# The input projection of a two-layer trunk in three sections of columns, its weights in quarters

## The chip, the cores and the metric

The kernel runs on one core of one Trainium2 chip. The metric is the device time of one execution in microseconds (us); smaller is better. On the core, TensorE (PE in the profile) multiplies matrices, VectorE (DVE), ScalarE (ACT) and GpSimd (POOL) work element by element, and SyncE (SP) issues most of the DMA transfers. Each engine takes its instructions strictly in the order in which they stand in its own queue.

## What is computed

The reference is a trunk of two layers. Each layer mixes tokens with four groups of heads side by side (latent attention, neighbourhood attention "natten", a bidirectional S5 state space model, and retention) and then runs a mixture of experts. There are 512 latent and 256 context tokens, 1024 wide. What matters here is one product in each layer: the normed tokens times `w_in`, whose columns feed all four mixers.

```
hl = rmsnorm(x)   * (1 + scale) + shift      # 512 latent tokens, 1024 wide
hc = rmsnorm(ctx) * (1 + scale) + shift      # 256 context tokens
pl = split_cols(hl @ w_in[layer])            # cq 192 | ckv 128 | kr 32 | natten q,k,v | u | retention q,k,v,g
pc = split_cols(hc @ w_in[layer])
...
s5: state h[t] = abar * h[t-1] + bbar u[t], both directions; y = Re(c h) + d u; gelu; gated by w_glu
```

## The kernel before

**Tokens and columns.** A tile of tokens is 128 rows; there are six (`NT`), four latent and two context. The 1376 columns that are wanted with tokens on the partitions (`nat_ps` in the profile) are made in five sections, `SECS = (0, 288, 560, 832, 1104, 1376)`. `proj_nat(s, ...)` (line 515) makes one section: for each tile of tokens it accumulates 8 slices of the contraction (`KD`, 128 each) in one bank of PSUM, three matmuls for each slice, because the product is made from a high and a low part of each operand (`mm3`, lines 201 to 203). That is 24 matmuls for a tile and section; the number of columns in the section is the number of columns that each matmul streams. In layer 1 the context tokens need no queries, so their tiles begin at a later column: at `N_KR` in section 0 (32 columns), at `N_NV` in section 1 (80 columns), and at the section's start elsewhere. The remaining columns (u, and natten's q and k, and retention's gate) are made transposed (`tr_ps`, `proj_tr`): u before the sections, the others after them.

**Weights.** `wload` (line 488) brings one half of a section's weights, 512 of the 1024 rows of the contraction, into `w_raw`; `wnext` (line 499) casts it on ACT (`w_hi`, line 195), takes the rest by a subtraction on POOL (`w_lo`, line 196), and issues the load of the same half of the next section. There are three buffers of `w_raw` and four each of `w_hi` and `w_lo`, so two whole sections fit: the next one is ready while one is used.

**What is done with a section's tile.** DVE or ACT copies it out of PSUM (`evac`, lines 189 and 191). For cq and ckv there is a normalisation: ACT squares and sums, DVE makes `rs_a` (line 223), POOL makes `rs_b` (line 225), DVE scales into `acn` (line 1038), PE transposes that (`a_t`, lines 1041 and 1043). Three banks of PSUM serve `nat_ps` and `tr_ps`.

**S5 among the sections.** `s5_states` (line 763) is emitted after section 0 and `s5_out` after section 2 (`S5AT`). `s5_states` first makes the inputs of a scan with 64 small matmuls (`s5_v`, line 777), for which eight tiles `Fg` are loaded into two buffers. ACT copies them into `H`, and then DVE runs the scan: 56 operations on 192 columns (lines 789 to 792), 88 on 16 columns (797 to 800), 8 on 1232 columns (805 to 808). When it ends, ACT copies `H` to `HP` (lines 814 to 816). `s5_out` multiplies `HP` with tables (`s5_y`, lines 835 to 837; 92 of its 96 matmuls stand behind the first use of `HP`), copies to `Y`, loads a table and applies gelu on ACT (839), writes `Y` to memory and reads it back as `GT` (842, 844), DVE adjusts it (845), and PE multiplies it with `w_glu` (`s5_z`, line 857).

**What sets the order.** A scheduler in the framework orders the instructions of each engine when the program is built, by its own model of cost, within what the data and buffers allow. So the position of an instruction in its queue is fixed then, and a changed tile size moves other instructions too.

Of the kernel before, what the change touches and what calls it, by code (L numbers as in the profile page):

```python
# [9 lines left out]
F32 = mybir.dt.float32  # L10
F32R = mybir.dt.float32r
# [7 lines left out]
P = 128  # L19
# [14 lines left out]
SECS = (0, 288, 560, 832, 1104, 1376)  # L34
# [95 lines left out]
N_RQ, N_KR, N_CQ, N_NV, N_CKV, N_NW, N_RK, N_RV = 0, 256, 288, 480, 560, 688, 864, 1120  # L130
# [3 lines left out]
_ORDER = ("rq", "kr", "cq", "nv", "ckv", "nw", "rk", "rv", "u", "nq", "nk", "rg")  # L134
# [29 lines left out]
class Trunk:  # L164

    NB = ((7, 4, 3), (7, 6, 0))
    S5AT = ((0, 2), (0, 2))
# [156 lines left out]
    def mixer(self, l):  # L324
        tc, nc = self.tc, self.nc
        nt = self.nt
        with ExitStack() as left, ExitStack() as right:
            mS = self.pool("mS", es=left)
            self.mxS = mS.tile([P, 2, 2, nt * P], F32R, name="mixS")
            with ExitStack() as proj:  # L330
# [44 lines left out]
                with ExitStack() as sx:  # L375
                    na = self.pool("na", 2, es=sx, side="right")
                    self.s5u = self.pool("s5u", es=sx, side="right")
                    w = self.wnext()
                    self.s5_in(w, natP, self.s5u)
                    self.mla_prep_load(na)  # L380
                    for s in range(5):
                        self.proj_nat(s, na, tabs)
                        if s == self.S5AT[l][0]:
                            for _ in tabs:
                                pass
                            tb.close()
                            s5p, s5w = self.pool("s5p", es=sx, side="right"), self.pool("s5w", 2, es=sx, side="right")
                            self.s5_states(s5p, s5w)
                        if s == self.S5AT[l][1]:
                            self.s5_out(s5p, s5w)  # L390
# [97 lines left out]
    def wload(self, c0, w, a):  # L488

        r = self.W.tile([P, 4, w], F32, tag="raw", name="w_raw", bufs=3)  # L490
        o = c0 * D + a * 512 * w
        self.nc.sync.dma_start(out=r.rearrange("p k n -> p (k n)"), in_=self.I["w_in"][self.l, o:o + 512 * w].rearrange("(p n) -> p n", p=P))
        return r

    def wstart(self):
        self.secs = [(T_U, 256)] + [(a, b - a) for a, b in zip(SECS[:-1], SECS[1:])] + [(T_NK, 256), (T_RG, 256), (T_NQ, 256)]
        self.ahead = [self.wload(*self.secs[0], a) for a in range(2)]

    def wnext(self):

        w = self.secs.pop(0)[1]
        his, los, ahead = [], [], []
        for a in range(2):
            hi = self.W.tile([P, 4, w], F32R, tag="whi", name="w_hi", bufs=4)
            lo = self.W.tile([P, 4, w], F32R, tag="wlo", name="w_lo", bufs=4)
            self.split(hi, lo, self.ahead[a], self.nc.gpsimd)
            if self.secs:
                ahead.append(self.wload(*self.secs[0], a))
            for k in range(4):
                his.append(hi[:, k])  # L510
                los.append(lo[:, k])
        self.ahead = ahead
        return his, los

    def proj_nat(self, s, na, side):
# [5 lines left out]
        for i in range(NT):  # L521

            a = c0 if (i < LAT or self.need_ctx) else (N_KR, N_NV, c0, c0, c0)[s]
# [6 lines left out]
            next(side, None)  # L530
            next(side, None)
            for p0, w, dst in ((N_RQ, 256, self.nat[:, i, 0]), (N_KR, 32, None), (N_CQ, 192, None), (N_NV, 80, 0), (N_CKV, 128, None),
# [11 lines left out]
                elif dst is None:  # L544
                    g = self.mla_prep(i, p0, src, na)
                    next(g)
                    self.later.append(g)
                else:
                    self.evac(dst[:, x0 - p0:x1 - p0], src)

# [1328 lines left out]
def _layout(i):  # L1879
# [7 lines left out]
    r["w_in"] = np.concatenate([w[:, :, x:y].reshape(L, 2, 4, P, y - x).transpose(0, 1, 3, 2, 4).reshape(L, -1) for x, y in zip(cuts[:-1], cuts[1:])], axis=-1)  # L1887
# [40 lines left out]
```

## Time and profile before

| | us |
|---|---|
| median of three runs (2271.03 to 2276.7) | 2274.34 |
| the profiled execution | 2264.39 |
| span of its trace | 2262.6 |
| PE busy in the span | 1965.2 (87%) |
| DVE busy | 944.2 (42%) |
| POOL busy | 366.5 (16%) |
| the 1440 matmuls of nat_ps, busy | 146.6 + 144.0 + 144.2 |
| layer 0: first nat_ps matmul to first natten score | 89.94 to 297.15 |
| layer 1: the same | 1284.62 to 1476.61 |

Times inside the execution are counted from the start of the span. The profiled execution is 10 us below the median. A matmul's busy time in the trace includes the part in which the next one already runs, so what a row of matmuls takes is read from starts, not from busy times.

### The profile page before, as it was taken

How to read it: one execution, taken by the hardware profiler on the slowest of the kernel's cores; microseconds unless marked ns; L12 is line 12 of the kernel's file. 1: busy time of each engine (PE TensorE's matmuls, PEld its weight loads, DVE VectorE, ACT ScalarE, POOL GpSimd, SP SyncE). 2: the span in 40 equal slices, each digit the busy share in tenths (PEclk: the TensorE clock that was granted, in tenths of full speed). 3: DMA queues.
4: the chain of work that ended last, by engine and by line, in shares of the span. 5: the costliest groups of instructions: out<-in, count | busy, mean ns of one | idle time of the engine just before them, and what ended most of it. 6: DMA issues, size and time to landing. Idle time of an engine off the chain costs nothing. (4 is left out here: it accounts for less than half of the span.)

```text
span 2262.6 us, 32559 instructions
## 1 busy us (share of the span) xinstructions
PE 1965.2 (87%) x12449; PEld 1157.3 (51%) x12449; DVE 944.2 (42%) x2178; ACT 502.9 (22%) x1099; POOL 366.5 (16%) x396
## 2 busy tenths in 40 slices
PE   5887988899779899899887878988996999989996
PEld 2787765467633333333222778855574444444443
DVE  4757156463525411111112447166534444544445
ACT  3442232351202110000001432232522011111111
POOL 2431252220110000000003222262302000000000
PEclk8899999999879999999998989989996899999998
DMA  7441355753468999999998421365544899999996
GB/s 271 112 145 43 92 173 190 220 172 119 177 257 303 356 385 374 378 382 385 406 379 322 134 82 42 83 201 172 191 157 156 315 382 378 389 420 419 420 387 260
DMA packets 160476, 578.53 MB, mean 256 GB/s; under 512 B 30032, under 2 KB 71504, under 8 KB 111152
## 3 DMA queue, kind: packets, MB, share of 16 engines
q1 hardware_dynamic: 123344, 530.69, 62.0%
q10 hardware_dynamic: 31296, 31.36, 4.4%
q0 software_dynamic: 5664, 14.23, 2.2%
q8 instruction: 103, 1.69, 0.3%
q14 instruction: 69, 0.57, 0.1%
HBM read 536.33 MB, written 43.42 MB: 256 GB/s over the span
## 5 line engine op out<-in xcount | busy, mean ns | idle before, releaser
L1670 PE MATMUL e_pa<-ew,hT 128*64 128x512 f32 x1792 | 451.9, 605 | 36.1 <-DMA ew<-in_moe_w 29.9
L1670 PEld LDWEIGHTS e_pa<-ew,hT 128*64 128x64 f32 x1792 | 137.5, 139 | 312.7 <-issue 259.2
L1694 PE MATMUL e_py<-ew,aT 128*64 128x512 f32 x896 | 219.4, 625 | 10.1 <-DVE aT L1686 8.9
L225 POOL TENSOR_TENSOR rs_b<-rs_a,mhalf 128x1 f32<-128x1 f32 (+1 forms) x58 | 38.3, 660 | 854.6 <-PE po_ps L1639 513.5
L1675 ACT ACTIVATE sA<-e_pa 64x512 f32<-64x512 f32 x56 | 33.1, 591 | 597.8 <-PE e_pa L1670 580.7
L201 PE MATMUL nat_ps<-w_hi,hTh 128*128 128x272 f32 (+3 forms) x480 | 146.6, 305 | 8.3 <-ACT nat L189 6.5
L1676 DVE TENSOR_TENSOR sA<-sA,e_pa 64x512 f32<-64x512 f32 x56 | 38.6, 690 | 274.5 <-ACT sA L1675 273.9
L203 PE MATMUL nat_ps<-w_hi,hTl 128*128 128x272 f32 (+3 forms) x480 | 144.2, 300 | 0.0
L202 PE MATMUL nat_ps<-w_lo,hTh 128*128 128x272 f32 (+3 forms) x480 | 144.0, 300 | 0.0
L196 POOL TENSOR_TENSOR w_lo<-w_raw,w_hi 128x1024 fp32r<-128x1024 f32 (+2 forms) x36 | 90.2, 2517 | 231.0 <-DMA w_raw<-in_w_in 108.5
L1694 PEld LDWEIGHTS e_py<-ew,aT 128*64 128x64 f32 x896 | 62.1, 142 | 120.5 <-issue 105.0
L191 DVE COPY hT<-hg_t 128x256 f32<-128x256 f32 (+2 forms) x46 | 24.7, 537 | 199.8 <-PE e_pa L1670 166.3
L1556 POOL DMA_INDIRECT hg<-hd,stok x32 | 30.7, 960 | 443.8 <-PE hg_t L1568 368.4
L295 PE MATMUL mod_ps<-wmod,cT 128*32 128x256 f32 x768 | 77.0, 429 | 28.4 <-DMA wmod<-in_w_mod 28.4
L201 PEld LDWEIGHTS nat_ps<-w_hi,hTh 128*128 128x128 f32 x480 | 95.8, 200 | 10.5 <-ACT nat L189 7.9
L202 PE MATMUL tr_ps<-hTl,w_hi 128*128 128x256 f32 (+1 forms) x256 | 88.6, 346 | 10.0 <-POOL hTl L485 9.0
L202 PEld LDWEIGHTS nat_ps<-w_lo,hTh 128*128 128x128 f32 x480 | 95.7, 199 | 0.4 <-issue 0.4
L203 PEld LDWEIGHTS nat_ps<-w_hi,hTl 128*128 128x128 f32 x480 | 95.4, 199 | 0.2 <-issue 0.2
L201 PE MATMUL tr_ps<-hTh,w_hi 128*128 128x256 f32 (+1 forms) x256 | 88.2, 344 | 5.1 <-DVE gT L582 3.3
L203 PE MATMUL tr_ps<-hTh,w_lo 128*128 128x256 f32 (+1 forms) x256 | 85.8, 335 | 0.0
L1641 DVE TENSOR_TENSOR xr<-xr,po_ps 128x512 f32<-128x512 f32 x112 | 72.3, 684 | 7.9 <-PE po_ps L1639 7.4
L1016 PE MATMUL pT_ps<-const,sm_p 128*128 128x128 f32 x352 | 56.2, 286 | 18.4 <-DVE sm_p L1006 11.8
(471 smaller groups left out, 3495.3 us busy)
## 6 DMA issues: line engine op xcount, KB each, us to landing
ew<-in_moe_w SPq DMA_DIRECT2D x384, 1024.0 KB, 11.1
wmod<-in_w_mod SPq DMA_DIRECT2D x96, 512.0 KB, 4.5
yd<-zero SPq DMA_DIRECT2D x20, 512.0 KB, 5.0
w_raw<-in_w_in SPq DMA_DIRECT2D x16, 544.0 KB, 4.5
w_raw<-in_w_in SPq DMA_DIRECT2D x16, 512.0 KB, 3.2
w_raw<-in_w_out SPq DMA_DIRECT2D x32, 256.0 KB, 3.4
yd<-yA ACTq DMA_DIRECT2D x64, 128.0 KB, 6.1
hd<-h ACTq DMA_DIRECT2D x10, 512.0 KB, 2.6
```

Source lines behind the costliest of these rows:

```text
L196: (eng or self.nc.vector).tensor_tensor(out=lo, in0=src, in1=_f(hi), op=ALU.subtract)
L201: mm(out, lhsT=lh, rhs=rh, start=start, stop=False)
L202: mm(out, lhsT=lh, rhs=rl, start=False, stop=False)
L203: mm(out, lhsT=ll, rhs=rh, start=False, stop=stop)
L225: nc.gpsimd.tensor_tensor(out=r, in0=t, in1=self.mhalf[:, :n], op=ALU.pow)
L295: nc.tensor.matmul(ps[32 * j:32 * j + 32, 256 * q:256 * q + 256], lhsT=self.cT[:, k], rhs=w[:, j], start=(k == 0), stop=(k == KD - 1))
L1016: nc.tensor.transpose(pt[:, b], p[:, (a + b) * P:(a + b + 1) * P], self.ident)
L1641: nc.vector.tensor_tensor(out=x, in0=x, in1=ps, op=ALU.add)
L1670: mm(pa[64 * j:64 * j + 64], lhsT=hT[k][:, 0:64], rhs=(w1, w3)[j][k], start=(k == 0), stop=(k == KD - 1))
L1675: nc.scalar.activation(out=sA, in_=pa[0:64], func=AF.Silu)
L1676: nc.vector.tensor_tensor(out=sA, in0=sA, in1=pa[64:128], op=ALU.mult)
L1694: mm(py[64 * j:64 * j + 64, 0:512], lhsT=aT[:, k * 64:(k + 1) * 64], rhs=w2[k][:, h * 512:(h + 1) * 512], start=(k == 0), stop=(k == 3))
```

## The change

The five sections become three, of 464, 464 and 448 columns. The columns are put in another order: those of natten's w (`N_NW`, 176) move up beside `rq` and `kr`. In layer 1 the context tiles now stream 208, 272 and 448 columns where they streamed 32, 80, 272, 272 and 272.

Weights are loaded, cast and subtracted in quarters of the contraction, two slices each, four per section instead of two. `w_raw` keeps three buffers, `w_hi` has five and `w_lo` six, each half as deep and about 1.6 times as wide; so a section and one or two quarters fit, and not two sections. The generator that makes S5's tables between the tiles is advanced three times for a tile instead of twice. `s5_states` is emitted after tile 3 of section 0, `s5_out` after tile 4 of section 1.

```diff
-SECS = (0, 288, 560, 832, 1104, 1376)
+SECS = (0, 464, 928, 1376)
...
-N_RQ, N_KR, N_CQ, N_NV, N_CKV, N_NW, N_RK, N_RV = 0, 256, 288, 480, 560, 688, 864, 1120
+N_RQ, N_KR, N_NW, N_CQ, N_NV, N_CKV, N_RK, N_RV = 0, 256, 288, 464, 656, 736, 864, 1120
...
-    S5AT = ((0, 2), (0, 2))
+    S5AT = ((0, 3), (1, 4))
...
-        r = self.W.tile([P, 4, w], F32, tag="raw", name="w_raw", bufs=3)
-        o = c0 * D + a * 512 * w
+        r = self.W.tile([P, 2, w], F32, tag="raw", name="w_raw", bufs=3)
+        o = c0 * D + a * 256 * w
...
-        for a in range(2):
-            hi = self.W.tile([P, 4, w], F32R, tag="whi", name="w_hi", bufs=4)
-            lo = self.W.tile([P, 4, w], F32R, tag="wlo", name="w_lo", bufs=4)
+        for a in range(4):
+            hi = self.W.tile([P, 2, w], F32R, tag="whi", name="w_hi", bufs=5)
+            lo = self.W.tile([P, 2, w], F32R, tag="wlo", name="w_lo", bufs=6)
...
-            a = c0 if (i < LAT or self.need_ctx) else (N_KR, N_NV, c0, c0, c0)[s]
+            a = c0 if (i < LAT or self.need_ctx) else (N_KR, N_NV, c0)[s]
...
-            next(side, None)
-            next(side, None)
+            for _ in range(3):
+                next(side, None)
...
+            then(s, i)
```

`then(s, i)` holds the two calls that stood behind the sections: `s5_states` where `(s, i) == (0, 3)` and `s5_out` where `(s, i) == (1, 4)`. Lines behind the first edits move by one to four.

**PE, layer 0, where `HP` is first used.** `nat_ps` are section tiles, `tr_ps` the transposed ones behind all sections. Before:

```order
L203 MATMUL nat_ps_2480<-w_hi_2364,hTl_94 128x272
L201 MATMUL nat_ps_2480<-w_hi_2364,hTh_93 128x272
L202 MATMUL nat_ps_2480<-w_lo_2365,hTh_93 128x272
L836 MATMUL s5_y_2029<-HP_1503,Eg_2016 128x96
L203 MATMUL nat_ps_2480<-w_hi_2364,hTl_94 128x272
```

Now:

```order
L202 MATMUL tr_ps_2276<-hTh_93,w_hi_2252 128x512
L203 MATMUL tr_ps_2276<-hTl_94,w_hi_2252 128x512
L204 MATMUL tr_ps_2276<-hTh_93,w_lo_2253 128x512
L840 MATMUL s5_y_1855<-HP_1487,Eg_1842 128x96
L202 MATMUL tr_ps_2276<-hTh_93,w_hi_2258 128x512
```

Before, 40 section matmuls stood behind the first use of `HP`; now all sections stand ahead of it.

**DVE, layer 1, where the scan begins.** The first operation of the scan is the one that reads `H` and `s5pw1`. Before:

```order
L1038 TENSOR_SCALAR acn_11457<-nat_ps_11426,rs_b_11461 128x192
L191 COPY nv_11464<-nat_ps_11426 128x80
L223 TENSOR_SCALAR rs_a_11500<-ass_11497 128x1
L1038 TENSOR_SCALAR acn_11498<-nat_ps_11467,rs_b_11502 128x192
L789 TENSOR_TENSOR rt_11178<-H_11097,s5pw1_7513 128x192
```

Now:

```order
L1062 TENSOR_TENSOR kr_10442<-nat_ps_10784,k_krc_10647 128x32
L1064 TENSOR_TENSOR krt_10810<-nat_ps_10784,k_krs_10649 128x2x8 x2
L192 COPY nv_10816<-nat_ps_10784 128x176
L1065 TENSOR_TENSOR kr_10442<-kr_10442,krt_10810 128x32
L793 TENSOR_TENSOR rt_10906<-H_10825,s5pw1_7255 128x192
```

Before, the scan stood behind three tiles of section 1; now it stands behind the fourth tile of section 0, ahead of all of section 1.

**POOL, layer 1, towards the end of the scan.** The `memset` of `HP` waits for the scan's last operation. Before:

```order
L225 TENSOR_TENSOR rs_b_11808<-rs_a_11806,mhalf_59 128x1
L196 TENSOR_TENSOR w_lo_12195<-w_raw_12009,w_hi_12194 128x1088
L225 TENSOR_TENSOR rs_b_11847<-rs_a_11845,mhalf_59 128x1
L196 TENSOR_TENSOR w_lo_12201<-w_raw_12015,w_hi_12200 128x1088
L812 MEMSET HP_11367 64x16
```

Now:

```order
L226 TENSOR_TENSOR rs_b_11390<-rs_a_11388,mhalf_59 128x1
L197 TENSOR_TENSOR w_lo_11638<-w_raw_11176,w_hi_11637 128x896
L197 TENSOR_TENSOR w_lo_11644<-w_raw_11182,w_hi_11643 128x896
L197 TENSOR_TENSOR w_lo_11650<-w_raw_11188,w_hi_11649 128x896
L197 TENSOR_TENSOR w_lo_11825<-w_raw_11635,w_hi_11824 128x512
L816 MEMSET HP_11095 64x16
```

Three quarters of the last section (`w_lo_11638` and the two behind it) now stand behind the `rs_b` of the last latent tile of the section before, and directly ahead of the scan's end.

## Rows read from the trace of the kernel before

**Rows 1.** Stretches: us, busy us (instructions) by engine, clock, DMA share, GB/s.

```profile
152.70:216.70 64.00, 51.29 (x378) 49.17 (x378) 59.75 (x173) 11.87 (x35) 12.98 (x10) 0.97 0.23 73
219.80:265.90 46.10, 45.73 (x297) 41.18 (x298) 2.78 (x4) 13.59 (x18) 11.76 (x8) 1.00 0.37 92
...
1334.20:1399.80 65.60, 51.41 (x368) 50.21 (x368) 60.52 (x176) 12.47 (x41) 14.12 (x11) 0.87 0.17 51
...
1403.00:1476.00 73.00, 71.97 (x434) 62.81 (x434) 8.49 (x11) 21.12 (x31) 19.09 (x12) 1.00 0.32 83
```

**Rows 2.** What PE waited for, 89.9 to 297.2: total us, times, longest.

```profile
PE a_t L1041 <- DVE acn L1038: 6.7, 5, 2.5
...
PE s_t L727 <- DVE G L707: 3.4, 1, 3.4
```

**Rows 3.** The same, 1284.6 to 1477.

```profile
PE a_t L1041 <- DVE acn L1038: 11.9, 3, 8.5
PE s_v L777 <- DMA Fg<-s5f: 6.0, 2, 4.4
```

**Rows 4.** DVE, layer 0's scan: start, duration, operation, [idle before it, releaser].

```profile
152.76 0.51 DVE L789 TENSOR_TENSOR rt<-H,s5pw 128x192 f32<-128x192 f32 x1 [0.42 <-ACT H L782]
...
172.05 0.35 DVE L1038 TENSOR_SCALAR acn<-nat_ps,rs_b 128x128 f32<-128x128 f32 x1 [0.43 <-POOL rs_b L225]
172.32 2.58 DVE L792 TENSOR_TENSOR H<-H,rt 128x192 f32<-128x192 f32 x1
...
215.15 1.44 DVE L808 TENSOR_TENSOR H<-H,fx 128x1232 f32<-128x1232 f32 x1
```

**Rows 5.** POOL in order of time, the same moment.

```profile
172.00 2.49 POOL L196 TENSOR_TENSOR w_lo<-w_raw,w_hi 128x1088 fp32r<-128x1088 f32 x1
```

**Rows 6.** POOL's subtractions by shape: count, busy us, mean ns, idle before.

```profile
L196 POOL TENSOR_TENSOR w_lo<-w_raw,w_hi 128x1088 fp32r<-128x1088 f32 x16 | 41.2, 2585 | 34.0 <-ACT w_hi L195 34.0
L196 POOL TENSOR_TENSOR w_lo<-w_raw,w_hi 128x1024 fp32r<-128x1024 f32 x16 | 38.0, 2383 | 197.0 <-DMA w_raw<-in_w_in 108.5 <-ACT w_hi L195 70.8 <-PE nat_ps L203 10.4
```

**Rows 7.** PE in order of time: two first matmuls of tiles following each other.

```profile
212.96 0.29 PE L201 MATMUL nat_ps<-w_hi,hTh 128*128 128x272 f32 x1
215.98 0.29 PE L201 MATMUL nat_ps<-w_hi,hTh 128*128 128x272 f32 x1
1453.65 0.39 PE L201 MATMUL tr_ps<-hTh,w_hi 128*128 128x512 f32 x1
1459.09 0.39 PE L201 MATMUL tr_ps<-hTh,w_hi 128*128 128x512 f32 x1
```

**Rows 8.** PE, layer 1: first and last matmul of a tile of 32 columns.

```profile
1297.41 0.18 PE L201 MATMUL nat_ps<-w_hi,hTh 128*128 128x32 f32 x1
1299.90 0.26 PE L203 MATMUL nat_ps<-w_hi,hTl 128*128 128x32 f32 x1
```

**Rows 9.** DVE, start of layer 1's scan.

```profile
1334.26 0.55 DVE L789 TENSOR_TENSOR rt<-H,s5pw 128x192 f32<-128x192 f32 x1 [2.66 <-ACT H L782]
```

**Rows 10.** The tile Fg: last line of its page of instructions.

```profile
DMA to landing us min/median/max: 2.8/3.0/3.8
```

**Rows 11.** ACT and PE: from the last s5_y to s5_z in layer 0, and beyond.

```profile
248.38 0.48 ACT L838 COPY Y<-s_y 128x384 f32<-128x384 f32 x1 [6.62 <-PE s_y L837]
265.91 0.56 PE L857 MATMUL s_z<-GT,wglu 128*128 128x384 f32 x1 [0.38 <-DVE GT L845]
275.33 0.39 PE L201 MATMUL tr_ps<-hTh,w_hi 128*128 128x256 f32 x1 [3.32 <-DVE gT L582]
279.43 0.63 PE L201 MATMUL tr_ps<-hTh,w_hi 128*128 128x512 f32 x1
```

**Rows 12.** PE: first use of HP in each layer, and layer 1's first natten score.

```profile
219.76 0.43 PE L836 MATMUL s_y<-HP,Eg 128*128 128x96 f32 x2 [2.61 <-issue]
1402.96 0.32 PE L836 MATMUL s_y<-HP,Eg 128*128 128x96 f32 x1 [1.58 <-issue]
1476.61 0.48 PE L1146 MATMUL n_s<-nkT,nqT 64*128 64x256 f32 x1 [0.69 <-ACT nqT L587]
```

More of the change, by code (lines that the diff above doesn't have):

```diff
@@ L133 @@
                rq=(1376, 256), rk=(1632, 256), rv=(1888, 256), rg=(2144, 256))
-_ORDER = ("rq", "kr", "cq", "nv", "ckv", "nw", "rk", "rv", "u", "nq", "nk", "rg")
+_ORDER = ("rq", "kr", "nw", "cq", "nv", "ckv", "rk", "rv", "u", "nq", "nk", "rg")
 def _bc(ap, shape, axes):
@@ L380, in mixer, with then @@
                     self.mla_prep_load(na)
-                    for s in range(5):
-                        self.proj_nat(s, na, tabs)
-                        if s == self.S5AT[l][0]:
+                    def then(s, i):
+                        if (s, i) == self.S5AT[0]:
                             for _ in tabs:
@@ L386, in mixer @@
                             tb.close()
[L387 to L390, printed above, removed]
+                            self.s5p, self.s5w = self.pool("s5p", es=sx, side="right"), self.pool("s5w", 2, es=sx, side="right")
+                            self.s5_states(self.s5p, self.s5w)
+                        if (s, i) == self.S5AT[1]:
+                            self.s5_out(self.s5p, self.s5w)
+                    for s in range(len(SECS) - 1):
+                        self.proj_nat(s, na, tabs, then)
                 nat2 = self.pool("nat2", es=rt, side="right")
@@ L488, in wload @@
     def wload(self, c0, w, a):
-        r = self.W.tile([P, 4, w], F32, tag="raw", name="w_raw", bufs=3)
-        o = c0 * D + a * 512 * w
-        self.nc.sync.dma_start(out=r.rearrange("p k n -> p (k n)"), in_=self.I["w_in"][self.l, o:o + 512 * w].rearrange("(p n) -> p n", p=P))
+        r = self.W.tile([P, 2, w], F32, tag="raw", name="w_raw", bufs=3)
+        o = c0 * D + a * 256 * w
+        self.nc.sync.dma_start(out=r.rearrange("p k n -> p (k n)"), in_=self.I["w_in"][self.l, o:o + 256 * w].rearrange("(p n) -> p n", p=P))
         return r
@@ L496, in wstart @@
         self.secs = [(T_U, 256)] + [(a, b - a) for a, b in zip(SECS[:-1], SECS[1:])] + [(T_NK, 256), (T_RG, 256), (T_NQ, 256)]
-        self.ahead = [self.wload(*self.secs[0], a) for a in range(2)]
+        self.ahead = [self.wload(*self.secs[0], a) for a in range(4)]
     def wnext(self):
@@ L508, in wnext @@
                 ahead.append(self.wload(*self.secs[0], a))
-            for k in range(4):
+            for k in range(2):
                 his.append(hi[:, k])
@@ L513, in wnext, with proj_nat @@
         return his, los
-    def proj_nat(self, s, na, side):
+    def proj_nat(self, s, na, side, then):
         nc = self.nc
@@ L1886, in _layout @@
     cuts = SECS + (T_NQ, T_NK, T_RG, T_RG + 256)
-    r["w_in"] = np.concatenate([w[:, :, x:y].reshape(L, 2, 4, P, y - x).transpose(0, 1, 3, 2, 4).reshape(L, -1) for x, y in zip(cuts[:-1], cuts[1:])], axis=-1)
+    r["w_in"] = np.concatenate([w[:, :, x:y].reshape(L, 4, 2, P, y - x).transpose(0, 1, 3, 2, 4).reshape(L, -1) for x, y in zip(cuts[:-1], cuts[1:])], axis=-1)
     r["cc"] = np.stack([a["c"].reshape(KD, P).T, a["c_ctx"].reshape(KD, P).T], axis=-1)
```

## The prediction

> **What bounds the kernel now.** The change touches two stretches of the span, the projection of layer 0 (89.9 to 297.2 us) and of layer 1 (1284.6 to 1476.6), 399 us of 2262.6. I read first the busy time of each engine by stretch. Over the whole span PE is busy 87%, and one would look for PE's work; but in the stretch in which S5's scan runs, 152.7 to 216.7, DVE is busy 59.75 of 64.0 us and PE 51.29, and in layer 1 it is 60.52 of 65.6 against 51.41 [rows 1]. Behind the scan it turns round: from the first use of HP on, PE is busy 45.73 of 46.1 us, in layer 1 71.97 of 73.0. So each layer has two parts. Until HP is there, DVE's scan sets the time and PE waits for it in small pieces: 6.7 us for acn in layer 0 [rows 2], 11.9 us for acn in layer 1, with 6.0 more for the tables Fg that the scan's inputs need [rows 3]. After that, PE's queue sets the time, or the round trip from s5_y through ACT and memory to s5_z. The first use of HP comes at 219.76 and 1402.96, directly behind the scan's last operation at 215.15 + 1.44 in layer 0 [rows 4, 12]. The change can therefore gain in three places only: an earlier start of the scan, a shorter scan, or less PE work behind it.
>
> **Price of a matmul.** A tile is 24 matmuls, and its length is the difference of two tiles' first starts: 215.98 - 212.96 = 3.02 us with 272 columns, 126 ns each; 1459.09 - 1453.65 = 5.44 us with 512, 227 ns [rows 7]. That is 0.42 ns a column and about 12 ns besides; estimated from these, 464 columns take 207 ns and 448 take 200. With 32 columns a matmul still takes (1299.90 - 1297.41)/23 = 108 ns [rows 8], and I put 208 columns at 111. A layer drops 2 x 6 x 24 = 288 matmuls, 288 x 12 ns = 3.5 us. The Trainium skill ("TensorE: Matmul & The Clock Gate", section "Back-to-back issue gap") gives 2.5 ns beside the columns, which speaks against the change: by it 288 matmuls would be worth 0.7 us. The two rows do not agree with that figure.
>
> **Layer 0, start of the scan.** It waits for the last s5_v. Ahead of that stood 144 matmuls of 288 columns and 170 of 272, 40.6 us; by the order there will be 209 of 464, 43.2 us: +2.6. Before, PE lost some 5 us there, 3.4 of them for S5's tables on DVE [rows 2], beside which POOL then subtracted; now those subtractions come later, and it should lose some 1.6 us where section 0 begins (three quarters can be cast only as u's tiles release their buffers) and about 1 us where section 1 begins (three subtractions of 928, estimated at 2.1 us each from 2585 ns for 1088 and 2383 for 1024 [rows 6], against 1.24 us of PE per quarter; the scheduler covers most of it by running three tiles on the first quarter). Together 0, between -1 and +4; I take 0, since both large waits are short by the rows.
>
> **Layer 0, length of the scan.** Before it is 63.9 us, 152.76 to 216.59 [rows 4]. Between its operations now stand eight acn instead of five: each 0.35 us and the wait of 0.43 for rs_b [rows 4], 3 x 0.78 = +2.3. Copies out of PSUM are fewer but 448 wide: +0.6. Beside it POOL subtracts. One DVE operation, normally half a microsecond, took 2.58 us, from 172.32 on, while a subtraction ran from 172.00 to 174.49 [rows 4, 5], so DVE stood until it ended. Four fall in the scan before, two of 1088 and two of 1024 elements, six shorter ones now, three of 896 and three of 512, with 4224 elements in both. Counted by elements that is 0, counted by instruction (two more at 2 us) +4. I take the elements, because the row's operation ends half a microsecond behind the subtraction. The scan: +2.9, with ends -1 and +7. The Trainium skill ("SBUF — State Buffer", section "SBUF: two separate sides") says the same of a lock that DVE and GpSimd hold for a whole instruction; the row's 2.58 us agrees, and by the rule the term would be 0 too, where a price for each instruction would make the sum 4 us dearer.
>
> **Layer 0, behind the scan.** PE will have finished all sections by then, so it waits longer for HP, an estimated 10 to 20 us in two pieces instead of 2.61 [rows 12], and begins at half clock. After the 3.32 us wait at 275.33, 24 matmuls of 256 columns took 279.43 - 275.33 = 4.10 us instead of 24 x 0.12 = 2.9 [rows 11]; I put the same +1.2 here, between 0 and +3.5. From HP to s5_z it was 265.91 - 219.76 = 46.15 us. Now the last s5_y comes 28.9 us behind the first (18.6 us of tr_ps tiles and 92 s5_y at 112 ns), and the round trip takes 17.5 us, 248.38 to 265.91 [rows 11], of which PE's work covers only 10.7: 46.4, +0.2. What follows keeps its shape. PE's saving of 3.5 us falls into the wait for HP and is worth nothing. Layer 0: 0 + 2.9 + 1.2 + 0.2 = **+4.3 us**.
>
> **Layer 1, start of the scan.** Now it stands behind section 0's fourth tile. 1284.6 + 1.3 of waiting for quarters + 4 x 24 x 0.207 = 1305.7. Then the eight tables: two are there, the other six come in three pairs, each 3.0 us from issue to landing [rows 10] and 0.6 of s5_v and issue, and PE has only 0.7 us of other work between: 10.8 us more, some 6 of them idle, as many as before [rows 3]. With copies to H the scan starts at 1319 instead of 1334.26 [rows 9]: **-15**, between -11 and -16.
>
> **Layer 1, length of the scan.** 65.5 us before. One acn more, +0.8; smaller copies, -2.4; and POOL now subtracts eight quarters beside it, 6880 elements instead of 4352, since the last section's wait behind rs_b and run just ahead of the scan's end. If they block DVE as in [rows 4, 5] that is 2528 x 2.49/1088 = +5.8; if the long operations at the end run on, 0. I take +4.5. The scan: +2.9, HP 12 us earlier.
>
> **Layer 1, behind the scan.** Before, 134 matmuls of 272 columns stood behind the first s5_y, 16.9 us; now it is 123 of 448, 24.6: +7.7. s5_z stands 14.8 us of PE work behind the last s5_y, and the round trip takes 17.5: a wait of 2.7, where 1.0 was lost in that stretch: +1.7. Half clock after the wait: +1.2. Together +10.6 on 1476.61 - 1402.96 = 73.65 [rows 12]. Layer 1: -15 + 2.9 + 10.6 = **-1.5 us**. The narrower saving of the context tiles (28.7 to 21.0 us of PE) falls into PE's wait for acn, which grows to some 17 us after section 1's second tile, since six steps of the scan now stand ahead of its acn on DVE.
>
> **Sum.** +4.3 - 1.5 = +2.8 us on the profiled 2264.4, 2267. That execution is 10 us under the median of the runs, 2274.3, with which the result is compared; I add the sum to the median: **2277 us**, 0.1% slower. About 0.3%, 6.8 us, is what a measurement of this kernel can tell from no change.
>
> **Rivals.** *PE sets the pace after all.* The sum then is PE's work: 3.5 us in layer 0; in layer 1 89.9 - 79.8 = 10.1 us; 2274.3 - 13.6 = 2261. For it: PE is busy 80% even in the scan [rows 1], and the waits for acn are small pieces that the larger tiles might close. Against it: DVE's 93% in the same rows, and nothing in the change takes an operation off the scan. A half of it, with layer 0 unchanged and nothing but the matmuls added in layer 1, gives 2274.3 - 15 + 7.7 = 2267.
>
> *The quarters starve the scan in layer 0.* Two whole sections no longer fit, so casts wait for the running section's last tile, and POOL's three subtractions, behind the last kr copies, cost PE 3 to 4 us before the first s5_v; the scan starts at 156 or later. With six blocked operations counted by instruction (+4) this is 2277 + 4 + 4 = 2285. It decides from a start of the scan later than about 155.5. For it: POOL needs 2.1 us a quarter and PE 1.24. Against it: the order interleaves three tiles there.
>
> **How the numbers follow.** Forecast, within 0.3% on either side: 0.45. PE's pace, whole or half, beyond -0.3%: 0.25. Starved scan, or layer 1's end dearer, beyond +0.3%: 0.30. The likeliest case gives 2277; its own range, from the ends of its terms, is 2268 to 2284. The range for 8 in 10 goes to the rivals' times, 2261 to 2287. Faster 0.25, same 0.45, slower 0.30.
>
> **What would show it.** In the profile after: layer 0's first scan operation at 151 to 156, its last 66 to 67 us later with eight acn between; DVE above 90% there; a PE wait of over 5 us ahead of the first HP matmul. Layer 1's scan from about 1319, a PE wait for acn of 10 us or more in section 1, the first HP matmul near 1390, and the first natten score within 5 us of 1476 plus layer 0's shift. The forecast is wrong if the scan of layer 0 ends earlier than 215, if layer 1's end gains more than 5 us on its beginning, or if a stretch outside the projections moves by more than 3 us.

## The result: slower by 0.95%

The changed kernel takes **2295.19 us** (median of 4 runs, 2294.12 to 2296.9); the kernel before took 2275.52 beside it. The ratio of the runs is 1.0095, interval 1.0074 to 1.0115 (the medians alone are 0.86% apart). The forecast was 2277, within 0.3%, in a range up to 2287: the time lies above the range.

The profiled execution of the changed kernel spans 2291.9 us, that of before 2262.6. Between these two executions the 29.3 us come from four stretches, cut at the first matmul of a layer's first section and at the layer's first natten score: layer 0 up to its score +5.1, from there to layer 1's first section matmul +8.5, layer 1's projection +12.0, the rest +3.6. The second holds nothing of the change, and in the executions of the kernels below it varies from 987 to 1000 us whatever their edit. The two projections make 17.1 us of the 19.7 between the medians, and layer 1 most of it. There I had forecast -1.5.

The busy time of each engine by stretch, of the changed kernel: the scan and the piece from the first use of HP to s_z in layer 0, then the scan and the piece from HP to the first natten score in layer 1 (columns as in [rows 1], which these four answer).

```profile
154.40:217.90 63.50, 53.15 (x245) 46.89 (x245) 58.94 (x176) 14.27 (x47) 16.63 (x14) 0.92 0.15 38
221.10:268.80 47.70, 41.81 (x254) 36.96 (x254) 2.35 (x3) 12.99 (x19) 9.81 (x10) 0.94 0.43 112
1342.00:1413.50 71.50, 40.17 (x199) 34.12 (x198) 65.14 (x177) 16.32 (x51) 25.21 (x18) 0.81 0.18 54
1418.80:1502.30 83.50, 80.41 (x425) 69.04 (x423) 9.06 (x14) 21.13 (x36) 22.27 (x20) 1.00 0.36 98
```

The third row is the one to read. In layer 1's scan PE was busy 51.41 of 65.6 us before; now it is busy 40.17 of 71.5, at a granted clock of 0.81 instead of 0.87, while POOL is busy 25.21 instead of 14.12. In the fourth row PE is busy nearly throughout, for 83.5 us where it was 73.0: work that could not be done in the scan is done behind it.

What PE waited for in layer 1 of the changed kernel (it answers [rows 3]):

```profile
PE a_t L1045 <- DVE acn L1042: 21.6, 3, 12.2
PE s_v L781 <- DMA Fg<-s5f: 3.9, 5, 1.9
PE nat_ps L202 <- DVE kr L1065: 3.6, 1, 3.6
PE nat_ps L203 <- POOL w_lo L197: 3.6, 4, 1.7
PE a_t L1045 <- DVE bt L802: 2.3, 1, 2.3
```

And in layer 0 (it answers [rows 2]):

```profile
PE a_t L1045 <- DVE acn L1042: 9.8, 4, 5.0
PE s_z L861 <- DVE GT L849: 5.9, 1, 5.9
PE tr_ps L202 <- DVE gT L586: 4.0, 1, 4.0
PE s_y L840 <- ACT HP L820: 2.2, 1, 2.2
```

Layer 0's marks in order of time (they answer [rows 4, 11, 12]), and layer 1's (they answer [rows 9, 12]):

```profile
154.45 0.54 DVE L793 TENSOR_TENSOR rt<-H,s5pw 128x192 f32<-128x192 f32 x1 [2.35 <-ACT H L786]
221.11 0.43 PE L840 MATMUL s_y<-HP,Eg 128*128 128x96 f32 x2 [2.23 <-ACT HP L820]
268.80 7.67 PE L861 MATMUL s_z<-GT,wglu 128*128 128x384 f32 x16 [5.87 <-DVE GT L849]
302.30 0.70 PE L1150 MATMUL n_s<-nkT,nqT 64*128 64x256 f32 x2 [0.47 <-ACT nqT L595]
...
1298.28 0.38 PE L202 MATMUL nat_ps<-w_hi,hTh 128*128 128x464 f32 x1
1342.01 0.51 DVE L793 TENSOR_TENSOR rt<-H,s5pw 128x192 f32<-128x192 f32 x1 [14.08 <-ACT H L786]
1418.79 0.36 PE L840 MATMUL s_y<-HP,Eg 128*128 128x96 f32 x2
1502.31 0.70 PE L1150 MATMUL n_s<-nkT,nqT 64*128 64x256 f32 x2 [0.69 <-ACT nqT L591]
```

From the second half: the scan begins 43.7 us behind layer 1's first section matmul (before 49.6), HP is used first at 120.5 (before 118.3), the score comes at 204.0 (before 192.0). **The early scan did not make HP early**, and what stands behind HP is 9.9 us longer.

Two details show how. First, the scan's late start: SP, DVE and PE in order of time, between the third and the fourth tile of section 0.

```profile
1299.53 4.60 SPq L495 DMA_DIRECT2D w_raw<-in_w_in  x3
1304.18 8.68 SPq L835 DMA_DIRECT2D TPg<-s5k  x10
...
1313.40 0.47 SPq L853 DMA_DIRECT2D bglu<-in_s_b_glu  x1
...
1318.00 0.17 DVE L854 TENSOR_SCALAR bglu<-bglu 128x2 f32<-128x2 f32 x1 [19.09 <-DMA bglu<-in_s_b_glu]
...
1318.62 0.18 DVE L1065 TENSOR_TENSOR kr<-kr,krt 128x32 f32<-128x32 f32 x1
...
1318.85 0.73 PE L202 MATMUL nat_ps<-w_hi,hTh 128*128 128x464 f32 x1 [3.62 <-DVE kr L1065]
```

DVE's halving of b_glu, 0.17 us of work on two numbers, stands in its queue ahead of all of section 0's kr steps. Its load, 1 KB, stands on SP behind three loads of weight quarters, ten of TPg and one of w_glu. DVE sits idle for 19.09 us, section 0's tiles are not wholly read out of PSUM, and with its three nat_ps buffers full PE stops. Before, the same load came 13.4 us behind the first section matmul (now 15.1), and DVE waited 2.40 us for it, with the kr steps of two tiles already done. The late place of S5 has the wait too. The first two lines are of before, the third is of e5, a kernel of the next section.

```profile
1298.01 0.42 SPq L849 DMA_DIRECT2D bglu<-in_s_b_glu  x1
...
1300.53 0.17 DVE L850 TENSOR_SCALAR bglu<-bglu 128x2 f32<-128x2 f32 x1 [2.40 <-DMA bglu<-in_s_b_glu]
...
1309.40 0.17 DVE L854 TENSOR_SCALAR bglu<-bglu 128x2 f32<-128x2 f32 x1 [18.69 <-DMA bglu<-in_s_b_glu]
```

Second, inside the scan: DVE, POOL and PE in order of time.

```profile
1347.87 6.66 POOL L197 TENSOR_TENSOR w_lo<-w_raw,w_hi 128x928 fp32r<-128x928 f32 x3 [1.42 <-ACT w_hi L196]
...
1347.99 2.25 DVE L795 TENSOR_TENSOR rt<-rt 128x192 f32<-128x192 f32 x1
1350.27 2.37 DVE L796 TENSOR_TENSOR H<-H,rt 128x192 f32<-128x192 f32 x1
1352.48 2.33 DVE L794 TENSOR_TENSOR rt<-H,s5pw 128x192 f32<-128x192 f32 x1
...
1373.09 0.42 DVE L1042 TENSOR_SCALAR acn<-nat_ps,rs_b 128x192 f32<-128x192 f32 x1 [0.41 <-POOL rs_b L226]
...
1373.57 0.47 PE L1045 MATMUL a_t<-const,acn 128*128 128x128 f32 x1 [12.23 <-DVE acn L1042]
...
1400.51 10.16 POOL L197 TENSOR_TENSOR w_lo<-w_raw,w_hi 128x896 fp32r<-128x896 f32 x4 [0.79 <-ACT w_hi L196]
...
1409.89 0.45 PE L1045 MATMUL a_t<-const,acn 128*128 128x128 f32 x1 [8.02 <-DVE acn L1042]
```

Each subtraction on POOL (6.66 us for three) holds one DVE operation for its whole length: 2.25, 2.37 and 2.33 us for steps that take 0.36 to 0.6. And section 1's first acn stands on DVE behind 48 of the scan's 56 operations on 192 columns, 31 us behind the scan's start; PE has then been waiting for it for 12.23 us.

### The profile page after: what moved, and what is told of

It reads as the page before. It is cut to its first block, busy times and chain, and to the rows that moved or that the text cites. A ratio compares the mean times of both kernels' runs of the same rounds, so it can differ in the third digit from the quotient of the medians.

```text
span 2291.9 us, 31443 instructions
## 1 busy us (share of the span) xinstructions
PE 1971.5 (86%) x11873; PEld 1134.7 (50%) x11873; DVE 933.8 (41%) x2172; ACT 505.6 (22%) x1113; POOL 374.5 (16%) x416
## 5 line engine op out<-in xcount | busy, mean ns | idle before, releaser
L197 POOL TENSOR_TENSOR w_lo<-w_raw,w_hi 128x512 fp32r<-128x512 f32 (+2 forms) x56 | 98.5, 1777 | 206.5 <-DMA w_raw<-in_w_in 102.7
L202 PE MATMUL nat_ps<-w_hi,hTh 128*128 128x464 f32 (+3 forms) x288 | 111.1, 386 | 6.2 <-DVE kr L1065 3.6
L203 PE MATMUL nat_ps<-w_lo,hTh 128*128 128x464 f32 (+3 forms) x288 | 110.8, 385 | 4.9 <-POOL w_lo L197 4.9
L204 PE MATMUL nat_ps<-w_hi,hTl 128*128 128x464 f32 (+3 forms) x288 | 109.4, 380 | 0.0
L192 DVE COPY hT<-hg_t 128x256 f32<-128x256 f32 (+2 forms) x46 | 24.7, 537 | 200.5 <-PE e_pa L1674 166.6
L1643 PE MATMUL po_ps<-Yh,ohT 128*128 128x512 f32 (+1 forms) x128 | 56.8, 450 | 16.9 <-DVE xr L1645 10.2
L1592 PE MATMUL g_ps<-hx,oh 128*128 128x512 f32 x224 | 58.1, 412 | 8.1 <-DVE oh L1585 8.1
L202 PEld LDWEIGHTS nat_ps<-w_hi,hTh 128*128 128x128 f32 x288 | 58.7, 204 | 12.9 <-issue 6.3
```

Source lines behind the costliest of these rows:

```text
L197: (eng or self.nc.vector).tensor_tensor(out=lo, in0=src, in1=_f(hi), op=ALU.subtract)
L202: mm(out, lhsT=lh, rhs=rh, start=start, stop=False)
L203: mm(out, lhsT=lh, rhs=rl, start=False, stop=False)
L204: mm(out, lhsT=ll, rhs=rh, start=False, stop=stop)
L1592: nc.tensor.matmul(pg, lhsT=oh[:, i, 0:P], rhs=self.hx[i][z][:, c], start=(i + z == 0), stop=(i == n - 1 and z == 1))
L1643: nc.tensor.matmul(ps[:, q * o - 512 * c:q * o - 512 * c + o], lhsT=ohT[:, (i * m + q) % 8], rhs=y[:, q * o:q * o + o], start=(z == 0), st ...
```

## The experiments

Eighteen kernels were run beside the kernel before. This table has layer 1 of each profiled execution in us behind that layer's first section matmul, read as in the marks above; "idle" is PE's idle time up to the first use of HP, "behind" the section matmuls that start after it (their columns), and "us" is the median of the runs. The ratio is to the runs of the kernel before that were taken beside that kernel; their medians lie between 2271.9 and 2275.5 us, so small differences go by the ratios.

| kernel | scan starts | scan lasts | first HP | idle | behind | score | us | ratio [95%] |
|---|---|---|---|---|---|---|---|---|
| before | 49.6 | 65.5 | 118.3 | 22.7 | 134 (272) | 192.0 | 2275.5 | |
| changed | 43.7 | 71.5 | 120.5 | 40.0 | 123 (448) | 204.0 | 2295.2 | 1.0095 [1.0074, 1.0115] |
| e1 b_glu early | 37.5 | 71.6 | 113.8 | 35.5 | 123 (448) | 200.2 | 2298.0 | 1.0098 [1.0064, 1.0132] |
| e2 S5 late | 57.8 | 63.3 | 124.3 | 24.9 | 10 (448) | 190.1 | 2278.3 | 1.0007 [0.9991, 1.0023] |
| e3 quarters only | 41.9 | 65.4 | 110.5 | 16.2 | 153 (272) | 188.2 | 2266.3 | 0.9961 [0.9943, 0.9979] |
| e4 places only | 50.5 | 65.9 | 119.6 | 20.6 | 134 (272) | 193.6 | 2275.3 | 0.9999 [0.9974, 1.0025] |
| e5 layer 1 late | 57.0 | 63.4 | 123.6 | 23.9 | 10 (448) | 187.4 | 2275.6 | 1.0001 [0.9980, 1.0023] |
| e6 no subtraction | 45.3 | 58.2 | 109.0 | 24.7 | 123 (448) | 196.5 | 2264.9 | 0.9941 [0.9917, 0.9965] |
| e7 quarters, early | 42.0 | 65.3 | 110.9 | 15.5 | 153 (272) | 186.7 | 2265.0 | 0.9945 [0.9927, 0.9963] |
| e8 quarters, b_glu | 41.2 | 65.2 | 109.6 | 13.3 | 153 (272) | 186.7 | 2267.2 | 0.9961 [0.9940, 0.9982] |
| e9 acn on ACT | 43.7 | 66.2 | 114.9 | 33.3 | 115 (448) | 200.9 | 2285.9 | 1.0056 [1.0034, 1.0079] |
| e10 e7, acn on ACT | 42.4 | 61.3 | 106.9 | 15.4 | 169 (272) | 193.2 | 2273.6 | 1.0003 [0.9983, 1.0024] |
| e11 before, no subtr. | 49.8 | 56.3 | 109.3 | 12.5 | 123 (272) | 183.9 | 2248.1 | 0.9892 [0.9849, 0.9934] |
| e12 e5, no subtr. | 50.1 | 57.1 | 110.3 | 16.0 | 12 (448) | 173.3 | 2241.0 | 0.9859 [0.9816, 0.9903] |
| e13 steps on ACT | 44.8 | 64.9 | 112.9 | 35.5 | 115 (448) | 202.3 | 2289.6 | 1.0059 [1.0034, 1.0083] |
| e14 states early | 41.3 | 71.5 | 117.5 | 39.6 | 123 (448) | 200.6 | 2294.6 | 1.0095 [1.0061, 1.0128] |
| e15 output early | 54.6 | 63.4 | 121.1 | 25.0 | 9 (448) | 185.9 | 2274.9 | 1.0003 [0.9982, 1.0024] |
| e16 output last | 42.1 | 71.7 | 140.0 | 37.5 | 24 (448) | 208.7 | 2296.8 | 1.0106 [1.0067, 1.0144] |
| e17 both freed | 43.1 | 65.5 | 127.0 | 30.4 | 24 (448) | 195.3 | 2281.6 | 1.0041 [1.0023, 1.0059] |
| e18 e17, b_glu early | 38.5 | 65.2 | 122.8 | 27.3 | 24 (448) | 191.7 | 2278.4 | 1.0017 [0.9996, 1.0038] |

**Which part of the change costs?** Four kernels: the changed one with b_glu's load and halving moved to the start of S5's input (e1) or with both of S5's places put late (e2), and the one before with the quarters alone (e3) or with early places alone (e4).

```diff
e1 (s5_in, removed from s5_out)
+        self.bg = bg = sp.tile([P, 2], F32, name="bglu")
+        nc.sync.dma_start(out=bg, in_=self.I["s5_b_glu"][l]...)
+        nc.vector.tensor_scalar(out=bg, in0=bg, scalar1=0.5, ...)
e2
-    S5AT = ((0, 3), (1, 4))
+    S5AT = ((0, 5), (1, 5))
e3 (SECS and the order of the columns as before; 2 x 128 rows a load)
+    S5AT = ((0, 5), (2, 5))
e4 (SECS, columns and halves as before)
+    S5AT = ((0, 3), (2, 4))
```

> The changed kernel, with the small load of the bias bglu and its halving on DVE moved to the start of each layer's projection. Theory A (in layer 1 this load stands on SP behind section 1's weight loads, which wait for POOL, and DVE's halving of it stands ahead of all of section 0's copies, so PSUM fills and PE stops): PE's wait of 3.6 us for kr in layer 1 goes, the fourth tile runs at full clock, the scan starts about 6 us earlier in its stretch, and the time falls from 2295 to 2288-2290. Rival B (the scan's start is set by its tables and the wide tiles alone): the wait goes but the scan starts within 1 us of where it did, 2294-2296.

> The changed kernel, with the S5 stages emitted after the last tile of sections 0 and 1 instead of after tile 3 and tile 4. Theory A (the cost lies in the sections' width and in the queues, not in where S5 stands): the tables Fg are then waited for beside tiles of 464 columns, the scan of layer 1 starts later by some 3 us at most, 2293-2300. Rival C (the early place of S5, with only narrow context tiles between its table loads, is what costs): layer 1's scan starts as early or earlier, and the time falls to 2280-2286.

> The kernel before with its five sections, its order of columns and its places of S5, but weights in quarters with five and six buffers. Theory D (quarters starve PE and push SP's and POOL's queues): most of the loss is here, 2287-2297. Rival E (the sections' width is what costs: work left behind HP and DVE's order): 2272-2279, the time before.

> The kernel before with five sections and halves; only the S5 stages moved, the states to after tile 3 of section 0, the output to after tile 4 of section 2. Theory C (an early place of S5 is what costs, since layer 1's tables then come between narrow tiles): 2280-2290. Rival (an early start of the scan gains when the sections stay narrow, since more tiles then run beside the scan): 2262-2272.

e1: in the trace the wait for kr is gone and the scan starts 6.3 us earlier, as its theory has it; HP comes 6.7 earlier, but the score only 3.8, and the median does not fall as forecast (2298, with 5 runs from 2283 to 2303, in which a gain of 4 us would not show). The load explains the late start, not the lost time. e3 is 0.39% *faster* than before, against both its readings: the quarters are a gain, with PE's wait for Fg down from 6.0 us [rows 3] to 1.6 and the scan 7.8 us earlier. e4 changes nothing; in layer 1 only the two narrow context tiles lie between its place of the states and that of before. e2 takes back 17 of the 20 us, although its scan starts 14.1 us later, which neither of its readings had: the loss hangs on S5's early place in wide sections.

**In which layer, and is it POOL?** e5 puts S5 late in layer 1 alone. e6 is the changed kernel, e11 the one before and e12 is e5, each with the subtraction replaced by a memset (the raw weights are then free as soon as ACT has cast them). e7 is e3 with early places, e8 is e3 with e1's edit.

```diff
e5
-    S5AT = ((0, 3), (1, 4))
+    S5AT = (((0, 3), (1, 4)), ((0, 5), (1, 5)))   # by layer
e6, e11, e12
-            self.split(hi, lo, self.ahead[a], self.nc.gpsimd)
+            self.nc.scalar.copy(out=hi, in_=self.ahead[a])
+            self.nc.gpsimd.memset(_f(lo), 0.0)
e7 (on e3)
+    S5AT = ((0, 3), (2, 4))
```

> After, with S5's places given by layer: layer 0 keeps the early places (states behind section 0's fourth tile, output behind section 1's fifth), layer 1 has both behind its section's sixth tile. Theory F (the loss is layer 1's early scan, which runs ahead of nearly all of section 1, while in layer 0 the early place costs little): layer 1's first natten score 190 us (187 to 193) behind its first projection matmul instead of 204, layer 0's 213 to 216 as in the changed kernel, total 2279 to 2284. Rival (the early place costs in both layers): 2287 to 2292, with layer 1's score above 195.

> After, with the low part of the input projection's weights set to zero by a memset on POOL, and the high part by ACT's copy as before: POOL's subtractions (2 to 3 us each beside the scan) are left out, and the low parts of the weights are left out of the result; the matmuls and the loads are all still there, and a raw quarter is released by the copy on ACT alone. Theory G (the subtractions stretch the scan, each making a DVE operation as long as itself): layer 1's scan 62 to 65 us instead of 71.5, layer 0's 56 to 60 instead of 63.4, PE's waits for acn and kr shorter, total 2280 to 2287. Rival (the scan is long because it has more of the sections' DVE work in it, and the subtractions only fill gaps): both scans within 1.5 us of the changed kernel's, total 2292 to 2297.

> The kernel before with weights in quarters (five sections, the old order of columns) as in the run of the quarters alone, and S5's states behind the fourth tile of section 0, its output behind the fifth tile of section 2. Theory C (an early S5 costs nothing where sections are narrow, with halves or with quarters; it costs with sections of 464): 2262 to 2271, the same as the quarters alone. Rival (with quarters the early place costs whatever the sections' width, since six or more subtractions then fall into the scan): 2275 to 2283.

> The kernel before with weights in quarters, and the load and halving of b_glu moved from the states' code to the start of S5's input, so that neither stands behind the weights' loads on SP nor ahead of the kr copies on DVE. If b_glu's wait costs only where S5 stands early (theory A): at most 2 us less than the quarters alone, 2262 to 2268. If a wait of that kind is hidden in the narrow sections too and costs: 2256 to 2262, layer 1's scan starting 3 us or more earlier.

e5 is level with before: all of the loss is layer 1's place. Its time is even below what its theory asked, and its score as forecast. The same two stretches of e5, its scan and the piece from HP on, and its first use of HP:

```profile
1347.10:1410.50 63.40, 53.12 (x263) 47.09 (x262) 58.58 (x176) 13.08 (x44) 12.72 (x12) 0.95 0.10 28
1413.70:1477.50 63.80, 59.41 (x310) 49.44 (x310) 6.24 (x9) 21.30 (x34) 20.71 (x18) 0.96 0.39 102
...
1413.70 0.50 PE L840 MATMUL s_y<-HP,Eg 128*128 128x96 f32 x1 [4.79 <-issue]
```

The scan starts 13.3 us later and PE is busy 53.12 us in it instead of 40.17. HP comes only 3.1 us later, and 113 fewer matmuls of 448 columns, 23 us at 206 ns, stand behind it.

e6 gains 30 us, and both scans shrink (layer 1's to 58.2). That looked like the subtractions as the cause, so e11 and e12 asked the same of the other kernels.

> The kernel before with the low part of the input projection's weights set to zero by a memset on POOL in place of the subtraction, which leaves the low parts out of the result; all loads and matmuls are there. The changed kernel gained 30 us by that edit. If the subtractions are what makes the change dearer (theory G, more of them beside the scan): the kernel before gains 10 to 16 us only, 2258 to 2265, level with the changed kernel without them. If they cost both kernels alike, and the change's loss has another cause: 2242 to 2250, 15 to 23 us below the changed kernel without them.

> S5 early in layer 0 and late in layer 1, as in the run of that name (2276), with the low part of the weights by a memset on POOL, so that the low parts are left out of the result. It tells whether the 20 us that the early place costs in layer 1 need the subtractions. If they do (theory G): 2260 to 2268, the same as the early place without subtractions (2265). If the early place costs for another reason (PE standing at acn, section work behind HP): 2243 to 2252.

They gain 24 and 35 us by the same edit: the subtractions cost every version, and the early place in layer 1 costs 0.8% without them too (ratios 0.9941 against 0.9859), where it costs 0.9% with them (1.0095 against 1.0001). They lengthen the scan, but they are not why this change loses. Without them HP is used at 109.0 early and 110.3 late, and 123 matmuls stand behind it instead of 12.

e7 and e8 equal e3: with narrow sections neither the place nor b_glu matters. Of the versions that compute the whole result e7 has the lowest median, 2265.0 and 0.55% below before; e3 and e8 are level with it.

**Is it DVE's queue?** PE's largest waits are for acn. e9 scales acn on ACT (with the small step ahead of it on POOL), e10 does that to e7.

```diff
...
-        r = self.rsqrt(aw, ss, 1, 1.0, "ar")
-        nc.vector.tensor_scalar(out=t[:, :w], in0=ps[:, :w], scalar1=r, ...)
+        r = self.rsqrt(aw, ss, 1, 1.0, "ar", nc.gpsimd)
+        nc.scalar.activation(out=t[:, :w], in_=ps[:, :w], func=AF.Identity, scale=r)
```

> After, with acn's scaling on ACT instead of DVE and the small step rs_a ahead of it on POOL (whose rs_b follows), so that nothing of acn stands in DVE's queue among the scan's operations. Theory H (PE's waits for acn, 21.6 us in layer 1 of the changed kernel, come from acn's place behind six scan steps on DVE, and the scan itself is stretched by DVE's waits for rs_b): acn waits under 8 us in layer 1 and under 5 in layer 0, layer 1's scan 64 to 67 us instead of 71.5, its first natten score 190 to 196 us behind its first projection matmul instead of 204, total 2272 to 2283. Rival (the acn waits are only where PE stands for PSUM banks and the scan anyway; the work left behind HP is what costs): the waits move to kr, nat or HP, score at 200 or more, total 2289 to 2296.

> Quarters with five sections and S5's early places, as in the run of that name, with acn's scaling on ACT and rs_a on POOL. PE waits for acn there 11.2 us in layer 1 and 7.1 in layer 0, in many small pieces. Theory H: half of these go and the scans are 3 to 5 us shorter each: 2252 to 2260. Rival (with narrow sections PE's waits merely move to the next step of the scan's chain): 2261 to 2267.

What PE waited for in layer 1 of e9:

```profile
PE nat_ps L202 <- DVE nat L192: 12.2, 1, 12.2
PE a_t L1045 <- ACT acn L1042: 7.9, 2, 6.9
```

The wait for acn fell and the scan is 5.3 us shorter, as the theory has it; but a plain copy out of PSUM now holds PE as long as acn did, and the score stays at 200.9, as the rival has it. The median gains 9 us of 20, between the two; the edit works in both layers, and in the traces 4.5 us of the gain lie in layer 0's projection and 3.1 in layer 1's. e10 missed on the other side: HP is 4.0 us earlier than in e7 but 10.5 us more lies between HP and the score, and its median is 8.6 us higher.

So e13 takes all that layer 1's sections need of DVE off it; `evac` with (2, 2) sends every copy to ACT, with (1, 2) every second one. e14 and e15 separate the two places.

```diff
e13 (on e9, in layer 1 alone; nat, nv and the context's kr copies too)
...
-                    self.evac(dst[:, x0 - p0:x1 - p0], src)
+                    self.evac(dst[:, x0 - p0:x1 - p0], src, *((2, 2) if self.l else (1, 2)))
...
e14 / e15 (layer 1's entry; both on the changed kernel)
+    ((0, 3), (1, 5))  /  ((0, 5), (1, 4))
```

> After, with all that the sections need of DVE in layer 1 on ACT instead: acn's scaling (its small step rs_a on POOL), the copies nat and nv out of PSUM, and the context tiles' kr copies. Layer 0 is as in the changed kernel. In the run with acn alone on ACT, PE stood 12.2 us for a nat copy that DVE held back, in place of 12.2 us for acn. Theory Q (PE idles in layer 1 because steps of the sections that it needs stand behind the scan's operations in DVE's fixed order, whichever step that is): between the start of the scan and HP PE idles 12 to 16 us instead of 31.3, the first natten score stands 186 to 193 us behind the first projection matmul instead of 204, total 2274 to 2283. Rival (POOL's late quarters or ACT's queue take over): idle stays above 22 us, score at 197 or more, total 2286 to 2296.

> After, with S5's output in layer 1 behind section 1's sixth tile instead of its fifth, and its states behind section 0's fourth tile as in the changed kernel. If the states' early place makes the loss (theory Q, the scan put ahead of section 1 in DVE's order): first natten score 200 to 206 us behind the first projection matmul, total 2290 to 2298. If it is the output's place, whose matmuls stand between section 1's tiles on PE: score at 187 to 193, total 2274 to 2283.

> After, with S5's states in layer 1 behind section 0's sixth tile instead of its fourth, and its output behind section 1's fifth tile as in the changed kernel. Theory Q: first natten score 186 to 193 us behind the first projection matmul, total 2273 to 2281, as with both late (2276). If the output's place makes the loss: score at 198 or more, total 2288 or more.

e14 and e15 are clear: the states' early place makes the whole loss, the output's none. e13 refuted its theory: the idle time from the scan's start to HP (29.0 us), the score and the total came as its rival has them, but PE stood at another place than it named. PE in order of time, e13:

```profile
1383.18 0.36 PE L203 MATMUL nat_ps<-w_lo,hTh 128*128 128x448 f32 x1
1407.35 0.71 PE L840 MATMUL s_y<-HP,Eg 128*128 128x96 f32 x2 [23.81 <-issue]
```

Little of the sections holds PE now. It runs to 1383.5, meets the first s5_y that needs HP, and stands there for 23.81 us with 115 of section 2's matmuls still behind it in its order. The idle time has only changed its name: 40.0 us up to HP in the changed kernel, 33.3 with the wait at a copy, 35.5 with the wait at HP.

e16 puts the output behind section 2's fifth tile, which leaves 24 matmuls behind HP. e17 does that to e13, e18 adds e1's edit.

```diff
e16 (changed kernel) and e17 (e13), layer 1's entry
-    ((0, 3), (1, 4))
+    ((0, 3), (2, 4))
```

> After, with S5's output in layer 1 behind section 2's fifth tile instead of section 1's fifth; its states stay early, all else is as in the changed kernel. By the order 24 of section 2's matmuls stand behind the first use of HP on PE, where the changed kernel has 123. Theory R (two things each keep PE idle: section work that PE's order puts behind HP, and section steps that DVE's order holds behind the scan; freeing one lets the other hold): little changes, first natten score 196 to 203 us behind the first projection matmul, total 2287 to 2296. Rival S (PE's order alone makes the loss): score 183 to 189, total 2272 to 2281.

> Both edits in layer 1: the sections' DVE steps on ACT, and S5's output behind section 2's fifth tile. Theory R: PE idles at most 14 us between the start of the scan and HP (31.3 in the changed kernel, 29.0 with the steps on ACT alone), the first natten score stands 176 to 185 us behind the first projection matmul, total 2262 to 2273. If ACT's queue or POOL's quarters hold PE instead: idle above 20 us, total 2280 or more.

> As the run with both freed, and the load and halving of b_glu moved to the start of S5's input. If HP is then what PE waits for last in layer 1, its 6 us earlier scan shows in full: score 170 to 180, total 4 to 7 us below the run with both freed. If PE's own work is the limit once both are free: within 3 us of that run.

e16 gains nothing, as its theory said (though score and time lie above its ranges): the work stands ahead of HP now, but DVE's order still holds its acn. What PE waited for in layer 1 of e16:

```profile
PE a_t L1045 <- DVE acn L1042: 21.9, 3, 12.6
```

e17, with both freed, gains 14 us; I had expected 22 to 33, and its idle time from the scan's start to HP, 22.4 us, and its total are those of its rival, ACT's queue. What holds PE then, in ACT's order and PE's:

```profile
1404.66 1.46 ACT L818 COPY HP<-H 64x1520 f32<-64x1520 f32 x1 [23.54 <-DVE H L812]
...
1411.02 1.39 ACT L190 COPY nat<-nat_ps 128x448 f32<-128x448 f32 x3
...
1411.59 0.74 PE L202 MATMUL nat_ps<-w_hi,hTh 128*128 128x448 f32 x1 [16.09 <-ACT nat L190]
```

Now ACT's copies to HP wait 23.54 us for the end of the scan, and the copies out of PSUM stand behind them. e18's median is 3 us lower still, which its interval does not separate from e17. No complete version with wide sections and early states comes below the kernel before.

**What is shown.** The loss is layer 1's early states in wide sections (e2, e5, e14 against e15). It works through fixed orders: the sections' work cannot fill the scan, because it is put behind HP on PE, behind the scan on DVE, or behind HP's copies on ACT, and lifting one hold lets the next hold (e9, e13, e16, e17). **What stays open:** a version in which all three are lifted was not built, nor the late place with b_glu early, though e5 has that wait too. Of the 9 us that the quarters gain in five sections, the traces show 4 in layer 1 and a loss of 2 in layer 0, with 6 behind layer 1's first natten score; no cause was found for these 6, and that last stretch varies from 781 to 797 us in the executions of the other kernels. Three sections with halves were not tried, so what the width alone does is not shown.

## Why the prediction was wrong

**The views were read rightly.** DVE's scan and then PE's queue set the time, and a matmul's price nearly held: in tiles without waits 210 ns for 464 columns and 206 for 448, forecast 207 and 200. PE is busy 160.9 us in layer 1's projection, 6.8 less than before, where 10.1 had been forecast for its work. The dearer columns make 1.4 us of that difference (an estimate from these prices); the rest was not separated, but the granted clock over the projection was 0.90, before 0.92. And PE idles 43.1 us instead of 24.3.

**Layer 1, start of the scan: the step that failed most.** -15 forecast, -5.9 measured. The sum went over matmuls and Fg loads and left out two rows of `s5_out` that the scheduler puts into section 0: the load of b_glu and its halving on DVE. They stood there in the trace of before, where DVE waited 2.40 us for the load; now the halving stands ahead of all kr steps and DVE waits 19.09. The price is 6.3 us (e1). The s5_v chain behind it took 15.4 us instead of the forecast 13.3, at a granted clock of 0.89. But this step does not make the loss alone. In e1 the start is at -12.2, near the forecast, and the projection is still 8.2 us longer than before, since the other terms run dearer: +6.0 for the scan, +1.6 from its end to HP and +12.8 behind HP.

**Layer 1, length of the scan: mis-sized.** +2.9 forecast, +5.9 measured. Eight subtractions fall in, as counted, and the last four take POOL 10.16 us beside the long operations at the end. Their term held: without them the scan lasts 58.2 us instead of 71.5 (e6), before 56.3 instead of 65.5 (e11), so they cost 4.1 us more than before, booked at +4.5. The mis-sized term is the rest, one acn more and the copies: -1.6 booked, +1.9 measured by the same two runs. From the scan's end to HP 2.2 us more were lost, booked at nothing. So HP came 2.2 us *later* than before, where 12 earlier was the forecast.

**Layer 1, behind the scan: right, and the real loss.** +10.6 forecast, +9.9 measured, with 123 matmuls behind HP as counted; the 1.2 us booked for half clock did not come, the granted clock was 1.00. The error was one of judgment: I booked this as a cost beside a gain of 12 us. But even with b_glu early, HP is only 9.8 us earlier than in the late place (e1 against e5), while 23 us more stands behind it, and the score comes 12.7 us later.

**The wait for acn** was foreseen (17 us, measured 21.6) and put down as covered by the context tiles' saving. It is part of the idle time that was not covered: PE stood still while 123 section matmuls were left for the time behind HP.

**Layer 0: the sum right by luck, its terms not.** +4.3 forecast, +5.1 measured. The projection began 2.8 us earlier (87.13), which was not foreseen; with quarters alone it does so too (e3, 86.49). So the scan started at 154.45, inside the bounds, but 4.5 us later behind the first section matmul, where 0 was forecast and +4 was the upper end. It lasted 63.4 us instead of the forecast 66.8. HP came 1.35 us later than before, s_z a further 1.5, through a wait of 5.9 us for GT, and the rest to the score 2.3, where nothing was booked. PE's wait ahead of HP was 2.2 us, not 10 to 20: most of its idle time fell into acn's waits, 9.8 us.

**The rivals.** The starved scan gave the right sign, but its place was layer 0, where POOL's quarters cost PE 1.3 us. Layer 1's end, named beside it, was not dearer than booked. The miss lies ahead of HP: 9.1 us at the scan's start, 3.0 in its length and 2.2 from its end to HP. PE's pace did not come.

## What to carry to other kernels

Before a long serial step is moved forward, count what its move puts *behind* its result on the engine that consumes it: the end is the result's time plus that work, and an earlier start pays only if the result comes earlier by more than that. Follow every small line that is placed there too, down to a load of two numbers, and look at whose queue each stands in. When a wait is removed and the same idle time returns under another name, suspect the order of the queues before the operation that the profile names.

## What the runs showed of the hardware

- A subtraction on POOL and a DVE operation of two inputs held each other in both directions: DVE's 0.36 us step took 2.25 beside one, and a subtraction of 896 elements took up to 3.37 us beside DVE's long operations, where one of 928 elements with DVE idle took 2.23. DVE's copies of 448 columns out of PSUM took 0.62 us beside one and without. Beside memsets of the same tiles (e6) DVE's steps kept their 0.36 to 0.56 us. The Trainium skill ("SBUF — State Buffer", section "SBUF: two separate sides") puts the lock between a DVE operation with two SBUF inputs and a GpSimd operation that reads SBUF; both traces agree.
- PE's long wait cost time behind it too: after the 12.23 us for acn, 24 matmuls of 464 columns from 1375.68 on took 285 ns each, at a granted clock of 0.74; the next 24, from 1383.90 on, took 214 ns at 1.00. Over the whole scan the clock was 0.81 with PE busy 40 of 71.5 us, and 0.95 in e5 with 53 of 63.4.
